# The ends of two attention mixers: when the last row sums are spread, by which way one of them goes, and which PSUM banks two late products use

## The chip, the cores and the metric

The kernel runs on one core of a Trainium2 chip. Each engine of the core (TensorE, here PE; VectorE, DVE; ScalarE, ACT; GpSimd, POOL; SyncE, SP) works through its own queue of instructions in order, and waits on semaphores for what the other engines and the DMAs deliver. The metric is the time of one execution on the device in microseconds (us); several runs are compared by their median.

## What is computed

The reference is a trunk of two layers over 1024 tokens of width 1024, in float32.

```python
for i in range(DEPTH):                      # DEPTH = 2
    h = rms_norm(x, norm_g[i])
    y = mixer_a(h, ...) if i == 0 else mixer_b(h, ...)
    x = x + y
    g = sigmoid(rms_norm(x, ple_norm_g[i]) @ ple_w_gate[i])
    x = x + g * (p[i] @ ple_w_proj[i])
return rms_norm(x, final_norm_g)
```

Both mixers have 16 heads of 64 columns. Each projects h to q, k, v and a gate, takes softmax(q k) v for each head, multiplies by silu(gate), and ends in an output projection. Mixer A attends within a window of 8 x 16 neighbours on a 16 x 64 grid, mixer B to all 1024 tokens, with four heads sharing one k and v and with norms and rotations on q and k. For this study only the very last part of each mixer matters: the softmax is left undivided through the product with v, and the sum over each row of exponentials is divided out of the result at the end.

## The kernel before

**Arithmetic.** Each float32 operand is split into a high and a low part, and a product is three matmuls (`split3`, recorded under the helper's line L321). Tokens come in 8 tiles of 128; a "half" hf is four of these tiles. The heads are worked in eight pairs.

**Four stages.** Mixer A, a dense phase (output projection in Strassen's form, `strassen_out`, then the gated projection), mixer B, and a dense phase again. The mixers use seven or eight of the eight PSUM banks in pools of their own, and the dense phase that follows takes the same eight banks afresh (four for its tiles `d`, four for `t`).

**Order of the work.** The order of all instructions is written out by hand. `mix` takes a list `att` of attention items and a list `dense` of projection items with costs, and puts dense items behind attention items so that both advance in proportion. After each attention item runs `pulse`, which moves weights along (`WQ.pump`) and counts down the list `post`: `post.add(n, f)` means that f is issued n pulses later. `later` does the same once per attention step. The last few dense items can be kept back (`hold`, HOLD = 2) and run after the last attention item, one pulse each; mixer B keeps three, of which one is used up during the last attention step. These kept items are the last of 16 "p products" (`pp_items`), which multiply the per-layer embedding by its projection: six matmuls into one PSUM bank, evacuated by ACT (L635), and stored to DRAM by a DMA from SP's queue (L636).

**Attention steps.** Mixer A has 128 steps (16 heads x 8 tiles), mixer B 128 steps (pair, half, head of the pair, tile; numbers 112 to 127 are the last pair). Step n issues the transposes of its exponentials (`f_T`: PE, then ACT L1283 for the high part PTh and DVE L1284 for the low part PTl in mixer B; L794, L799, L800 in mixer A), the exponential of a later step (`f_E`, ACT L1271 or L786, which also sums the row), the scores of a still later step (`f_S`; in mixer B DVE L1265 takes their minimum), and the product with v (`f_AV`, tile `o`; in mixer B every second step, with one PSUM bank for `o`).

**End of a head.** `head_end` (L500) runs when a head's half of `o` is complete. It issues the evacuation of `o` (ACT L548), one pulse later `join` (DVE L512), which adds the low part into Y and frees the `o` bank, and `norm` (L537), which takes reciprocals of the row sums (DVE L538, 128 x 4). The row sums lie along partitions and must be turned to lie along columns, in a 128 x 512 tile `rb`. There are two ways:

- pairs 0 to 6: `rows` (L514) transposes 128 x 32 on DVE (L516), then SP writes it to DRAM with four DMAs (L519) and reads it back, spread over the partitions, with two (L521).
- pair 7: `spread` (L524) copies the reciprocals into 128 x 512 on DVE (L525), and `across` (L528) turns that with four PE transposes (L531) into a PSUM bank (mixer A: a tile `t`; mixer B: the one bank of `o`). For the first half ACT copies the bank to `rb` (L534); for the second half it is read from PSUM.

`fin_last` (L560) then multiplies Y by the gate (DVE L561) and by the reciprocals (L565), and writes the last eighth of the dense phase's input as high (ACT L570) and low part (DVE L573). In mixer A both halves of pair 7 end after the last attention step; in mixer B the first half ends while the last eight steps run (its head ends at step 120), and the second after the last step.

**PSUM banks of the p products.** `dalloc` gives a `d` bank: mixer A has two, mixer B one. Scores have two tiles `s` (mixer A one bank each, mixer B two banks each).

Of the kernel before, what the change touches and what calls it, by code (L numbers as in the profile page):

```python
# [11 lines left out]
F32 = mybir.dt.float32  # L12
# [9 lines left out]
NT = 8  # L22
# [3 lines left out]
NH = 16  # L26
# [4 lines left out]
CA = (1.0, 0.5, 1.25, 1.0, 0.75)  # L31
CB = (1.25, 1.0, 2.0, 0.5, 1.0)
# [5 lines left out]
DT = (5, 2)  # L38
FIN = (4, 4)
HOLD = 2  # L40
# [120 lines left out]
def trunk(ctx, tc, x, wts, rpb, gains, hgains, mask, sides, rope, gain0, out):  # L161
    nc = tc.nc
    sync, act, dve, pool, pe = nc.sync, nc.scalar, nc.vector, nc.gpsimd, nc.tensor
# [154 lines left out]
    post = Later()  # L318
# [173 lines left out]
    def to_ht(pt, t, xn, cs=(0, 1)):  # L492
        for c in cs:
# [3 lines left out]
            act.activation(HTh[:, t, 4 * c:4 * c + 4], ps, AF.Copy)  # L497
            dve.tensor_tensor(HTl[:, t, 4 * c:4 * c + 4], ps, HTh[:, t, 4 * c:4 * c + 4], ALU.subtract)  # L498

    def head_end(sb, h, hf, rs, Ops, ylive, layer, gg, talloc):  # L500
        pair = h // 2
        b = (h % 2) * 64
        if h % 2 == 0:
            Y = sb.tile([128, 512], F32, name="Y", bufs=3 if layer == 0 else 2)
            rb = sb.tile([128, 512], F32, name="rb", bufs=2)
            r8 = sb.tile([128, 8], F32, name="r8", bufs=4)
            ylive[pair, hf] = (Y, rb, r8, {})
        Y, rb, r8, tail = ylive[pair, hf]
        yh = Y[b:b + 64]

        def join():
            dve.scalar_tensor_tensor(yh, Ops[0:64], 0.5, yh, op0=ALU.mult, op1=ALU.add)  # L512

        def rows():  # L514
            r8T = sb.tile([128, 32], F32, name="r8T", bufs=2)
            dve.transpose(r8T.rearrange("p (a c) -> p a c", a=4), r8[:, None].to_broadcast([128, 4, 8]))  # L516
            rD = dram.tile([8, 128], F32, name="rD", bufs=4)
            for b in range(4):
                post.add(DD[layer][1], lambda b=b: sync.dma_start(rD[:, 32 * b:32 * b + 32], r8T[32 * b:32 * b + 8]))  # L519
            for i in range(2):  # L520
                post.add(DD[layer][1], lambda i=i: sync.dma_start(  # L521
                    rb[64 * i:64 * i + 64], bass.AP(tensor=rD.tensor, offset=rD.offset + 512 * i, ap=[[0, 64], [1, 512]])))

        def spread():  # L524
            dve.tensor_copy(rb.rearrange("p (t j c) -> p t j c", t=4, j=2),  # L525
                            r8.rearrange("p (j t) -> p t j", j=2)[:, :, :, None].to_broadcast([128, 4, 2, 64]))

        def across():  # L528
            ps = talloc()
            for t in range(4):  # L530
                pe.transpose(ps[:, t], rb[:, t * 128:(t + 1) * 128], ident)  # L531
            ps = ps.rearrange("p t c -> p (t c)")
            if hf == 0:
                act.activation(rb, ps, AF.Copy)  # L534
            tail["rb"] = rb if hf == 0 else ps

        def norm():  # L537
            dve.reciprocal(r8[:, 4 * (h % 2):4 * (h % 2) + 4], rs)  # L538
            if h % 2 == 0:
                return  # L540
            if pair < 7:
                post.add(DD[layer][0], rows)
            else:
                spread()
                post.add(DT[hf], across)

# [12 lines left out]

        def fin_last():  # L560
            dve.tensor_tensor(Y, Y, G, ALU.mult)  # L561
            if "rb" not in tail:
                post.l = [e for e in post.l if e[1] is not across]
                across()
            dve.tensor_tensor(Y, Y, tail["rb"], ALU.mult)  # L565
            y3 = Y.rearrange("p (t c) -> p t c", t=4)
            ts = slice(4 * hf, 4 * hf + 4)

            def hi():
                act.activation(HTh[:, ts, 7, :], y3, AF.Copy)  # L570

            def lo():
                dve.tensor_tensor(HTl[:, ts, 7, :], y3, HTh[:, ts, 7, :], ALU.subtract)  # L573
            if hf == 0:
                post.add(3, hi)
                post.add(5, lo)
            else:
                hi()
                lo()

        def fin():
            yhi, ylo = rb.bitcast(F32R), Y.bitcast(F32R)

            def store(c, src):
                sync.dma_start(yD[layer][c][4 * hf:4 * hf + 4, :, pair, :].rearrange("t p c -> p t c"),
                               src.rearrange("p (t c) -> p t c", t=4))

            def split():
                act.activation(yhi, Y, AF.Copy)
                dve.tensor_tensor(ylo, Y, yhi, ALU.subtract)  # L590
                post.add(2, lambda: (store(0, rb), store(1, Y)))
            pool.tensor_tensor(Y, Y, G, ALU.mult)
            pool.tensor_tensor(Y, Y, rb, ALU.mult)
            if pair < 4 and hf == 1:
                post.add(YS[layer] + 2, lambda: store(0, Y))
            else:
                post.add(YS[layer], split)
        return fin_last if pair == 7 else fin
# [72 lines left out]
    def mixer_a():  # L671
        jobs = weight_sums()
        with ExitStack() as es:
# [6 lines left out]
            MK = one.tile([128, 5, 128], F32, name="MK")  # L680
            SIDE = one.tile([128, 3, 128], F32, name="SIDE")

            def dalloc():
                return pd.tile([128, 512], F32, name="d")

            def valloc():
# [2 lines left out]
            gg, ylive = {}, {}  # L689
# [69 lines left out]
            def f_S(h, j):  # L759
                k0, k1 = near(j)  # L760
                m = (k1 - k0 + 1) * 128
                n = 256
                ps = psS.tile([128, 512], F32, name="s")
                qt = QS[h][:, j * 128:(j + 1) * 128]
                ks = slice(k0 * 128, (k1 + 1) * 128)
                mm(ps[:, :m], qt, KA[h][:, ks], True, False)
                mm(ps[:, :m], qt, KB[h][:, ks], False, True)
                if j == 0:
                    RS[h] = sb.tile([128, 8], F32, name="rs", bufs=3)
                    tb = TB[h][:, 2:5:2]  # L770
# [12 lines left out]
            def f_E(h, j):  # L783
                n = 256
                sp, mn = SP[h, j]
                act.activation(sp[:, :n], sp[:, :n], AF.Exp, bias=mn, scale=-1.0, accum_out=RS[h][:, j:j + 1])  # L786

            def f_T(h, j):
                sp, _ = SP.pop((h, j))
# [199 lines left out]
            def open3():  # L989
                WQ.cap[3] = 1  # L990

            f_S(0, 0)
            f_E(0, 0)
            join(0)
# [3 lines left out]
            f_E(0, 1)  # L998
            f_S(0, 2)
            load_u(1)  # L1000
            steps = [(h, j) for h in range(NH) for j in range(NT)]

            def av_and_v(h, kb):
                fs = [(lambda: f_AV(h, kb), CA[4])]
# [4 lines left out]
            for h in range(NH):  # L1009
# [24 lines left out]
                    if h == 14 and j == OPEN3:  # L1034
                        att.append((open3, 0.0))
                if h == NH - 1:
                    att += [(lambda k=k: f_AV(NH - 1, k), CA[4]) for k in range(NT - 3, NT)]
                dense = []
                if h < NH - 1:
                    dense += qk_items(h + 1)  # L1040
# [13 lines left out]
    def mixer_b(pend):  # L1054
        with ExitStack() as es:
# [13 lines left out]
            def dalloc():  # L1069
                if pro[0]:  # L1070
                    pro[1] += 1
                    if pro[1] <= ENTRY:
                        return psS.tile([128, 1024], F32, name="s")[:, :512]
                    if pro[1] % 2 == 0:
                        return psO.tile([128, 512], F32, name="o")
                return pd.tile([128, 512], F32, name="d")

            gg, ylive = {}, {}
            KA, KB, V, QT, QST, P, RS, OP = {}, {}, {}, {}, {}, {}, {}, {}
            later = Later()  # L1080
# [187 lines left out]
            def f_E(h, hf, t):  # L1268
                ps, mn = P[h, hf, t]
                p = sb.tile([128, 1024], F32, name="P")  # L1270
                act.activation(p, ps, AF.Exp, bias=mn, scale=-1.0, accum_out=RS[h, hf][:, t:t + 1])  # L1271
                P[h, hf, t] = p

            def f_T(h, hf, t):
# [57 lines left out]
            for g in range(4):  # L1332
# [27 lines left out]
                    if YLOAD_B <= n < YLOAD_B + NT:  # L1360
                        att.append((lambda t=n - YLOAD_B: load_y(1, t), 0.0))
                if g == 3:
                    att.append((lambda: f_AV(*steps[-1]), CB[1]))
                def gates(p):
                    return [i for hf in range(2) for i in gate_items("bg", p, hf, dalloc, sb, gg)]
                dense = []
# [475 lines left out]
```

## Time and profile before

| | us |
|---|---|
| median of three runs | 1506.16 |
| lowest and highest run | 1504.79 and 1506.50 |
| profiled execution, device time | 1505.39 |
| its span from first to last instruction | 1503.6 |
| mixer A ends, first dense phase begins | about 517.7 in the span |
| mixer B ends, second dense phase begins | about 1323.1 in the span |

The profiled execution's own time is 1.8 us more than its span, and 0.77 us less than the median of the three runs.

How to read the profile: a row of the timeline gives start, duration, engine, line and operation, output tile <- input tiles, shape, and in square brackets how long the engine was idle before it and whom it waited for. `x2` means that consecutive instructions of the same kind are merged in one row. Matmuls are pipelined, so that their modelled durations overlap: six matmuls of 128 x 512, each shown with about 0.4 us, take about 1.4 us together. A row of the windows view gives, for one stretch of the span, the busy time of each engine with the number of instructions, the granted TensorE clock, the share of the DMA engines' time that was used, and GB/s.

### The profile page before, as it was taken

To read this page: it belongs to the slowest core of one execution; us is meant where nothing else is said; L and a number is where in the kernel's file an instruction comes from. 1 tells how busy PE (TensorE), PEld (TensorE's weight loads), DVE (VectorE), ACT (ScalarE), POOL (GpSimd) and SP (SyncE) were. 2 spreads that over 40 slices of the span, in tenths; PEclk is the share of its full clock that TensorE was granted. 3 is DMA by queue.
4 is the path that set the end of the run, shared out by engine and by line. 5 is a ranking of instruction groups with operands and counts; after the bars stand their busy time and mean duration, and the time that the engine had idled before them with its cause. 6 is when DMAs were issued, how large, how long until landed. Compare 5 with 4: busy or idle time off the path is not lost.

```text
span 1503.6 us, 24725 instructions
## 1 busy us (share of the span) xinstructions
PE 1480.6 (98%) x8885; PEld 1304.0 (87%) x8885; DVE 1071.6 (71%) x2042; ACT 917.2 (61%) x1866; POOL 461.0 (31%) x623
## 2 busy tenths in 40 slices
PE   8999999999999999999999999999999999999998
PEld 8888988988988887888988999989999988888886
DVE  7566476477477598756887786777877887689844
ACT  7676476477477535433567776767767777745432
POOL 1456476387265200020322222443131300000123
PEclk9999999999999999999999999999999999999999
DMA  8334374283122863262210111111101122763223
GB/s 257 126 104 131 71 178 139 64 168 100 36 89 85 326 247 99 92 206 80 77 50 22 33 51 39 47 33 44 58 28 48 38 78 66 240 234 114 69 90 135
DMA packets 91242, 157.44 MB, mean 105 GB/s; under 512 B 18160, under 2 KB 54256, under 8 KB 90608
## 3 DMA queue, kind: packets, MB, share of 16 engines
q1 hardware_dynamic: 87120, 143.53, 29.1%
q0 software_dynamic: 2560, 8.39, 3.7%
q10 hardware_dynamic: 1440, 3.94, 0.8%
q8 instruction: 71, 1.16, 0.3%
q14 instruction: 51, 0.42, 0.1%
HBM read 125.30 MB, written 50.83 MB: 117 GB/s over the span
## 4 chain that ended last, share of the span: by engine, by line
PE 51%; DVE 7%; ACT 2%; issue 1%; POOL 0%; ACTq 0%; POOLq 0%; DVEq 0%
PE d L321 25%; PE s L321 9%; PE o L321 8%; PE t L1281 7%; PE t L496 1%; DVE xn L1616 1%; PE t L321 1%; DVE X L1512 1%; DVE PTl L1284 1%; DVE HTl L1458 0%; DVE wl L235 0%; DVE mn L1265 0%; DVE wl L1410 0%; PE t L1235 0%; ACT wh L230 0%
## 5 line engine op out<-in xcount | busy, mean ns | idle before, releaser
L321 PE MATMUL d<-wh,HTh 128*128 128x256 f32 (+1 forms) x1000 | 331.8, 335 | 1.9 <-DVE X L1512 0.6
L321 PE MATMUL d<-wh,HTl 128*128 128x256 f32 (+1 forms) x1000 | 327.7, 331 | 0.4 <-DVE HTl L498 0.4
L321 PE MATMUL d<-wl,HTh 128*128 128x256 f32 (+1 forms) x1000 | 327.0, 330 | 0.3 <-DVE wl L1410 0.2
L1284 DVE TENSOR_TENSOR PTl<-t,PTh 128x512 fp32r<-128x512 f32 x256 | 164.7, 685 | 106.5 <-ACT PTh L1283 106.2
L321 PEld LDWEIGHTS d<-wh,HTh 128*128 128x128 f32 x1000 | 187.8, 189 | 22.2 <-ACT HTh L497 1.5
L321 PEld LDWEIGHTS d<-wl,HTh 128*128 128x128 f32 x1000 | 188.1, 189 | 20.0 <-DVE wl L1410 0.6
L321 PE MATMUL d<-HTh,wh 128*128 128x512 f32 x504 | 204.6, 406 | 0.0
L321 PEld LDWEIGHTS d<-wh,HTl 128*128 128x128 f32 x1000 | 187.9, 189 | 18.9 <-DVE HTl L498 0.6
L321 PE MATMUL d<-HTh,wl 128*128 128x512 f32 x504 | 198.1, 393 | 0.0
L321 PE MATMUL d<-HTl,wh 128*128 128x512 f32 x504 | 197.3, 392 | 0.0
L1271 ACT ACTIVATE P<-s,mn 128x1024 f32<-128x1024 f32 x128 | 142.7, 1115 | 47.3 <-DVE mn L1265 46.4
L1283 ACT ACTIVATE PTh<-t 128x512 fp32r<-128x512 f32 x256 | 139.2, 594 | 46.2 <-PE t L1281 45.7
L1265 DVE TENSOR_REDUCE mn<-s 128x1 f32<-128x1024 f32 x128 | 155.1, 1212 | 9.8 <-PE s L321 9.2
L804 POOL TENSOR_TENSOR PTh<-PTh,SIDE 128x256 fp32r<-128x256 f32 x96 | 81.2, 845 | 192.9 <-ACT PTh L799 192.9
L1281 PE MATMUL t<-ident,P 128*128 128x128 f32 x1024 | 134.8, 273 | 2.6 <-DVE PTl L1284 2.0
L321 PE MATMUL s<-KA,QS 128*128 128x512 f32 (+2 forms) x384 | 134.1, 403 | 1.1 <-DVE mn L778 1.1
L1281 PEld LDWEIGHTS t<-ident,P 128*128 128x128 f32 x1024 | 115.3, 140 | 12.8 <-DVE PTl L1284 6.9
L321 PE MATMUL s<-KB,QS 128*128 128x512 f32 (+2 forms) x384 | 121.5, 370 | 0.0
L235 DVE TENSOR_TENSOR wl<-wstage,wh 128x1024 fp32r<-128x1024 f32 x78 | 97.8, 1255 | 32.8 <-ACT wh L230 32.5
L321 PE MATMUL o<-PTl,V 128*128 128x256 f32 (+2 forms) x672 | 120.0, 290 | 1.1 <-DVE PTl L1284 0.6
L321 PE MATMUL o<-PTh,V 128*128 128x256 f32 (+2 forms) x672 | 118.4, 287 | 1.8 <-DVE Y L512 0.8
L321 PEld LDWEIGHTS d<-HTh,wl 128*128 128x128 f32 x504 | 94.6, 188 | 21.6
(253 smaller groups left out, 2883.3 us busy)
## 6 DMA issues: line engine op xcount, KB each, us to landing
wstage<-in_wts SPq DMA_DIRECT2D x88, 512.0 KB
pp<-ppD SPq DMA_DIRECT2D x32, 256.0 KB
X<-in_x SPq DMA_DIRECT2D x15, 512.0 KB
rb<-rD SPq DMA_DIRECT2D x56, 128.0 KB
ppD<-th SPq DMA_DIRECT2D x20, 256.0 KB
tD0t<-in_wts SPq DMA_DIRECT2D x16, 256.0 KB
tD1t<-in_wts SPq DMA_DIRECT2D x16, 256.0 KB
xD<-X SPq DMA_DIRECT2D x8, 512.0 KB
```

The source lines that it names most:

```text
L235: eng.tensor_tensor(lo[:, c:c + n], s[:, c:c + n], hi[:, c:c + n], ALU.subtract)
L321: pe.matmul(ps, a, b, start=first, stop=last, skip_group_check=True)
L496: pe.transpose(ps[:, k], xn[:, (4 * c + k) * 128:(4 * c + k + 1) * 128], ident)
L804: pool.tensor_tensor(pt[:, 3 * j - 1:3 * j + 4:4], pt[:, f1:f1 + 1].to_broadcast([128, 2, 128]), SIDE[:, :2], ALU.mult)
L1265: dve.tensor_reduce(mn, ps, axis=AX.X, op=ALU.min)
L1271: act.activation(p, ps, AF.Exp, bias=mn, scale=-1.0, accum_out=RS[h, hf][:, t:t + 1])
L1281: pe.transpose(ps[:, i], p[:, k * 128:(k + 1) * 128], ident)
L1283: act.activation(PTh[:, ks, c], ps, AF.Copy)
L1284: dve.tensor_tensor(PTl[:, ks, c], ps, PTh[:, ks, c], ALU.subtract)
L1512: dve.tensor_tensor(xt, ps, xt, op)
L1616: dve.scalar_tensor_tensor(xn, X[t], rn[m][:, i:i + 1], g1, op0=ALU.mult, op1=ALU.mult)
```

## The change

1. **Last row sums.** In both mixers, two pulses after the last exponential has been issued, `last_sums` takes the reciprocals of the last head's second half and spreads them into `rb`. `norm` then finds them there and only asks for `across`.
2. **Mixer B's last first half.** For pair 7, half 0 of mixer B, the row sums go the way of the pairs before it, through DRAM (`rows`); the copy L525, the four PE transposes L531 and the ACT copy L534 of this half are not issued.
3. **Banks of the kept p products.** Once the last product with v is reached, `dalloc` counts its calls: in mixer A the second kept p product gets a bank of the scores `s`, in mixer B the first and third do (with two left there, the first).

```diff
+    def last_sums(rs, ylive):
+        _, rb, r8, tail = ylive[NH // 2 - 1, 1]
+        dve.reciprocal(r8[:, 4:8], rs)
+        dve.tensor_copy(rb.rearrange("p (t j c) -> p t j c", t=4, j=2),
+                        r8.rearrange("p (j t) -> p t j", j=2)[:, :, :, None].to_broadcast([128, 4, 2, 64]))
+        tail["sums"] = True
+
     def head_end(sb, h, hf, rs, Ops, ylive, layer, gg, talloc):
...
         def norm():
+            if "sums" in tail and h % 2:
+                post.add(DT[hf], across)
+                return
             dve.reciprocal(r8[:, 4 * (h % 2):4 * (h % 2) + 4], rs)
             if h % 2 == 0:
                 return
-            if pair < 7:
+            if pair < 7 or layer == 1 and hf == 0:
                 post.add(DD[layer][0], rows)
+                tail["rb"] = rb
             else:
                 spread()
                 post.add(DT[hf], across)
```

In mixer A:

```diff
+            end = [0]
+
             def dalloc():
+                if end[0]:
+                    end[0] += 1
+                    if end[0] == 1 + HOLD:
+                        return psS.tile([128, 512], F32, name="s")
                 return pd.tile([128, 512], F32, name="d")
...
                 act.activation(sp[:, :n], sp[:, :n], AF.Exp, bias=mn, scale=-1.0, accum_out=RS[h][:, j:j + 1])
+                if (h, j) == steps[-1]:
+                    post.add(2, lambda: last_sums(RS[h][:, 4:8], ylive))
...
-                    att += [(lambda k=k: f_AV(NH - 1, k), CA[4]) for k in range(NT - 3, NT)]
+                    def last_av(k):
+                        end[0] = k == NT - 1
+                        f_AV(NH - 1, k)
+                    att += [(lambda k=k: last_av(k), CA[4]) for k in range(NT - 3, NT)]
```

In mixer B:

```diff
+                if end[0]:
+                    end[0] += 1
+                    if end[0] % 2 == 0:
+                        return psS.tile([128, 1024], F32, name="s")[:, :512]
                 return pd.tile([128, 512], F32, name="d")
...
                 act.activation(p, ps, AF.Exp, bias=mn, scale=-1.0, accum_out=RS[h, hf][:, t:t + 1])
+                if (h, hf, t) == steps[-1]:
+                    post.add(2, lambda: last_sums(RS[h, hf], ylive))
...
                 if g == 3:
-                    att.append((lambda: f_AV(*steps[-1]), CB[1]))
+                    def last():
+                        end[0] = 1
+                        f_AV(*steps[-1])
+                    att.append((last, CB[1]))
```

The list `steps` of mixer A is also built a few lines earlier than before, since `f_E` now reads it.

More of the change, by code (lines that the diff above doesn't have):

```diff
@@ L990, in open3 @@
                 WQ.cap[3] = 1
+            steps = [(h, j) for h in range(NH) for j in range(NT)]
             f_S(0, 0)
@@ L1000, in mixer_a @@
             load_u(1)
-            steps = [(h, j) for h in range(NH) for j in range(NT)]
             def av_and_v(h, kb):
@@ L1075, in dalloc @@
                         return psO.tile([128, 512], F32, name="o")
+                if end[0]:
+                    end[0] += 1
+                    if end[0] % 2 == 0:
+                        return psS.tile([128, 1024], F32, name="s")[:, :512]
                 return pd.tile([128, 512], F32, name="d")
+            end = [0]
             gg, ylive = {}, {}
```

## Prediction

> **What bounds the kernel now.** I read the page first, then the waits of PE over the whole span, then the timeline of both mixers' ends, and last the windows behind them.
>
> ```profile
> PE 1480.6 (98%) x8885; PEld 1304.0 (87%) x8885; DVE 1071.6 (71%) x2042; ACT 917.2 (61%) x1866; POOL 461.0 (31%) x623
> PE o L531 <- DVE Y L512: 0.8, 1, 0.8
> PE o L321 <- DVE Y L512: 0.8, 2, 0.5
> PE d L321 <- DVE X L1512: 0.6, 1, 0.6
> PE t L531 <- DVE rb L525: 0.5, 1, 0.5
> ```
>
> PE is busy for 1480.6 of 1503.6 us, so that all its gaps together are 23 us. The change can only take PE work away at one place (four transposes) and close gaps at the two ends. Two waits of the list belong to it by name, L531 on L512 (0.8) and L531 on L525 (0.5); shorter ones follow below. The whole matter is therefore one of one to three microseconds. The question for each is whether it is passed on to the end, or given back to DVE, which the Strassen stage behind each mixer keeps busy.
>
> **Part 1 and 3, mixer A.** The rows below are the timeline of its end: the last exponential, the first kept p product's last matmul, the spread of the second half's sums, its turn on PE, the second kept product, and the first product of the dense phase.
>
> ```profile
> 506.97 0.51 ACT L786 ACTIVATE sp<-sp,mn 128x256 f32<-128x256 f32 x1
> 509.31 0.42 DVE L800 TENSOR_TENSOR PTl<-t,PTh 128x256 fp32r<-128x256 f32 x1 [1.35 <-ACT PTh L799]
> 514.19 0.40 PE L321 MATMUL d<-wh,wl 128*128 128x512 f32 x1
> 514.47 0.43 DVE L525 COPY rb<-r 128x512 f32<-128x512 f32 x1
> 515.05 0.63 PE L531 MATMUL t<-ident,rb 128*128 128x128 f32 x4 [0.46 <-DVE rb L525]
> 515.43 0.48 PE L321 MATMUL d<-wh,KA 128*128 128x512 f32 x1
> 517.11 0.60 ACT L635 ACTIVATE G<-d 128x512 f32<-128x512 f32 x1 [1.88 <-PE d L321]
> 517.75 0.50 PE L321 MATMUL d<-wh,HTh 128*128 128x512 f32 x1 [0.25 <-ACT G L635]
> 519.17 0.69 DVE L565 TENSOR_TENSOR Y<-Y,rb 128x512 f32<-128x512 f32 x1 [2.85 <-ACT rb L534]
> 521.96 0.69 DVE L573 TENSOR_TENSOR HTl<-Y,HTh 128x512 fp32r<-128x512 f32 x1 [0.70 <-ACT HTh L570]
> 526.00:579.00 53.00, 52.36 (x229) 42.55 (x228) 52.31 (x77) 22.94 (x37) 0.00 (x0) 1.00 0.52 188
> ```
>
> The transposes start at 515.05 because the copy ends at 514.90. PE could have begun about a quarter of a microsecond behind the matmul of 514.19 (six such matmuls take 1.4 us), at 514.4. So the copy costs PE at least the 0.46 that the profile names and at most 515.05 - 514.4 = 0.65; I take 0.6, since the weights of the transposes were held up too.
>
> After the change the copy and its reciprocal come two pulses behind the exponential of 506.97, which is the last of the mixer. DVE then sits idle for 1.35 us before 509.31. The copy is 0.43, and a 128 x 4 reciprocal is at most the 0.20 that a 128 x 32 transpose takes below. Cover 1.35 against 0.63: they cost nothing. Without that cover, they would cost DVE at most 0.63 and PE nothing at that place, since PE's next product with v waits for other steps.
>
> The second kept product then starts 0.6 earlier, and with it all that hangs on its end in ACT's queue: its evacuation (517.11), a weight split, L534, and through it DVE's L565 at 519.17 (which waits 2.85 for L534), L570, and L573 at 521.96. From there DVE runs without a pause worth naming: 52.31 of the 53 us from 526 to 579. That run's start sets when the stage ends, and PE waits for it there (0.6 on L1512, above). So mixer A gives **0.6**.
>
> The other bank saves PE the wait of 0.25 at 517.75. Nothing else is held by it, and PE only reaches the end of DVE's run 0.25 earlier and waits there: I count **0**, with 0.25 to 0.4 as the upper end. That a p product in a scores bank waits for something new has no row; the last reader of these banks on ACT and DVE is before 508, and the product starts after 514, so that I take nothing for it, and as its upper end the 0.25 saved.
>
> **Part 2, mixer B's first half.** Here the turn on PE is removed. The timeline around it:
>
> ```profile
> 1289.41 1.03 PE L1281 MATMUL t<-ident,P 128*128 128x128 f32 x8
> 1290.54 0.68 DVE L512 SCALAR_TENSOR_TENSOR Y<-o,Y 64x512 f32<-64x512 f32 x1
> 1291.28 0.66 PE L531 MATMUL o<-ident,rb 128*128 128x128 f32 x4 [0.84 <-DVE Y L512]
> 1291.69 0.71 PE L321 MATMUL s<-KA,QS 128*128 128x512 f32 x2
> 1292.77 1.28 DVE L1284 TENSOR_TENSOR PTl<-t,PTh 128x512 fp32r<-128x512 f32 x2
> 1293.55 0.60 ACT L534 ACTIVATE rb<-o 128x512 f32<-128x512 f32 x1
> 1295.28 1.12 ACT L1271 ACTIVATE P<-s,mn 128x1024 f32<-128x1024 f32 x1 [0.37 <-DVE mn L1265]
> 1296.91 1.09 ACT L1283 ACTIVATE PTh<-t 128x512 fp32r<-128x512 f32 x2 [0.43 <-PE t L1281]
> 1300.78 1.29 DVE L1284 TENSOR_TENSOR PTl<-t,PTh 128x512 fp32r<-128x512 f32 x2 [0.81 <-ACT PTh L1283]
> 1301.98 1.22 DVE L1265 TENSOR_REDUCE mn<-s 128x1 f32<-128x1024 f32 x1
> 1303.83 0.69 DVE L565 TENSOR_TENSOR Y<-Y,rb 128x512 f32<-128x512 f32 x1
> 1306.34 1.29 DVE L1284 TENSOR_TENSOR PTl<-t,PTh 128x512 fp32r<-128x512 f32 x2 [1.82 <-ACT PTh L1283]
> 1310.16 1.19 PE L321 MATMUL o<-PTh,V 128*128 128x256 f32 x8 [0.52 <-DVE Y L512]
> ```
>
> PE waits 0.84 for the `o` bank, which L512 frees, and spends 1291.69 - 1291.28 = 0.41 on the transposes: the scores of step 123 can start **1.25** earlier. ACT loses L534 (0.60) and DVE a copy of 0.43; DVE gains a 0.20 transpose.
>
> Does PE keep the 1.25? The low parts of step 121 (1292.77) stand on DVE behind a weight split, and do not move; nor does the exponential of 1295.28, which waits for the minimum behind them. So ACT comes to L1283 of step 122 when that exponential ends, 0.43 earlier, not 1.25. DVE then works through low parts, minimum, low parts, minimum without its gap of 0.81 at 1300.78, and is 0.43 + 0.81 = 1.24 earlier at 1301.98. PE's own work in between is at no place nearer than that. At 1310.16 PE waits for DVE's L512 once more (0.52, the longer of the two of L321 above), and that L512 follows the same chain. So 1.2 of the 1.25 is left there: **1.2**.
>
> The DRAM way adds six DMAs to SP's queue, and L565 waits for their landing with all of DVE's queue behind it (the low parts of 1306.34 first). Its price by the pair before:
>
> ```profile
> 1260.28 0.20 DVE L516 STREAM_TRANSPOSE r8T<-r 128x32 f32<-128x32 f32 x1
> 1260.51 1.29 SPq L519 DMA_DIRECT2D rD<-r8T  x4
> 1263.38 1.09 SPq L521 DMA_DIRECT2D rb<-rD  x2
> 1267.15 1.30 POOL L593 TENSOR_TENSOR Y<-Y,rb 128x512 f32<-128x512 f32 x1 [6.85 <-DMA rb<-rD]
> 1260.50:1267.10 6.60, 6.60 (x40) 5.72 (x40) 3.51 (x4) 3.86 (x8) 0.00 (x0) 1.00 0.48 154
> 1290.80:1297.00 6.20, 5.72 (x38) 4.99 (x39) 3.98 (x5) 5.24 (x10) 0.00 (x0) 1.00 0.98 339
> ```
>
> From the first store to the use of rb: 1267.15 - 1260.51 = 6.6 us. The new transpose comes behind L512, which itself moves up by the copy's 0.43: 1290.54 - 0.43 + 0.68 + 0.20 = 1291.0, and the first store 0.2 later, at 1291.2. Landing by this row: 1297.8. But the DMA engines are at 0.98 there, against 0.48. If the share doubles the time, the landing is at 1291.2 + 13.2 = 1304.4; that is the upper end. L565 is reached at 1303.83 - 1.2 = 1302.6. I take 1299, nearer to the row, since most of the 6.6 us is the 2.87 between first store and first load and the 3.77 after, in which little data moves: **0**. On SP the loads hold the queue until about 1295, where the store of the next p product stands behind them; its data are ready about then (the evacuation of a product has to come after 1293.55 today), so it loses nothing worth counting. The Trainium skill, page DMA: Bandwidth & Descriptors, section Latency and other measured facts, gives an access to HBM as 0.2 us on average and 2 us at high load. By it, an estimate, both legs of this way could take 1.8 us longer here, with the landing at about 1301.4. No row shows the legs under such a load, and the sum is the same by the row and by the page.
>
> **Parts 1 and 3, mixer B's end.**
>
> ```profile
> 1317.29 1.29 DVE L1284 TENSOR_TENSOR PTl<-t,PTh 128x512 fp32r<-128x512 f32 x2 [1.10 <-ACT PTh L1283]
> 1320.90 0.66 PE L531 MATMUL o<-ident,rb 128*128 128x128 f32 x4
> 1320.97 0.60 ACT L635 ACTIVATE th<-d 128x512 f32<-128x512 f32 x1 [0.84 <-PE d L321]
> 1321.62 0.50 PE L321 MATMUL d<-wh,KA 128*128 128x512 f32 x1
> 1325.48 0.69 DVE L573 TENSOR_TENSOR HTl<-Y,HTh 128x512 fp32r<-128x512 f32 x1 [3.11 <-ACT HTh L570]
> ```
>
> The second half's sums move into DVE's gap of 1.10 before 1317.29 (0.63 of work). They are not late today: the turn at 1320.90 waits for L512 to free the bank. So **0**. The last p product needs the one `d` bank, which L635 holds until 1321.57; with the other bank it starts when the transposes end, 1320.90 + 0.41 = 1321.31: **0.3**. Its end sets ACT's next steps and L573, so DVE's start in the Strassen stage moves with it.
>
> **Sum.** 0.6 + 1.2 + 0.3 = 2.1 us. The profiled execution took 1505.39, so it would take 1503.3. It stands 0.77 below the median of the three runs; taken from the median, 1506.16 - 2.1 = **1504.1 us**, 0.14% less. About 0.2%, or 3.0 us, is what a measurement of this kernel can tell from no change (the three runs span 1.7), so my forecast is a gain below that.
>
> **The rivals.**
>
> *Swallowed in mixer B.* ACT and DVE between 1292 and 1310 could be no earlier at all, so that PE waits longer at 1310.16 and only 0.3 of B is left: 0.9 in all, 1505.3. For it: the exponential of 1295.28 does not move. Against it: the gaps of 0.43, 0.81 and 1.82 behind it, which are waits on PE or on its followers. 0.14.
>
> *All that is saved is kept.* In A 0.65 with the 0.4 of the bank, in B 1.4 and 0.35 with the pieces of other waits: 2.8 to 3.3, about 1503.1. Against it: the run of DVE from 526 to 579. 0.18.
>
> *Lost later.* The Strassen stage could be paced by something that does not move, a load landing. Then nothing is left: 1506.2. Against it: no wait of PE in the list names a DMA there. 0.08.
>
> *Slower: rb lands late.* Decided where L565 stands on DVE: from 1302.6 there are 1.8 us until the low parts of today's 1306.34, so a landing after 1304.4 moves everything behind it by what it is late, and after 1306.5 more is lost than the 2.1 gained. That is 15.3 us behind the first store, against 6.6 at half the DMA load. A landing at 1309 gives 2.5 slower, 1508.7. 0.08: the load of 0.98 speaks for it, the 4.8 us between 1297.8 and 1302.6 against.
>
> **How the numbers follow.** 0.52 is left for the forecast. A gain over 3.0 us needs the case where all is kept and half of its chance (0.09), or the forecast with a sixth of its chance for the scatter of medians (0.09), and 0.02 from the rest: faster 0.20. Slower by over 3.0: 0.05, most of the late landing. Within: 0.75. The range reaches down to 1503.1 less 1.1 of scatter, 1502.0, and up past the lost case, 1506.2 and 0.4: 1506.6; what it leaves out is mainly the late landing.
>
> **What would show it.** Right: no transposes L531 into `o` near 1290 and scores of step 123 right behind the transposes of step 121; no wait of L531 on L525; L573 of mixer A about 0.6 earlier and of mixer B about 2.1; PE's wait on L1512 behind mixer A 0.9 instead of 0.6. Wrong: DVE waiting for the DMA of rb at L565; a wait at 1310 of more than 0.7; a DVE run behind mixer A that begins earlier and ends where it did.

## The result, and the profile after

| | before | after |
|---|---|---|
| median, runs beside each other (22 of each), us | 1508.05 | 1504.69 |
| lowest and highest, us | 1504.79 and 1514.23 | 1503.08 and 1509.15 |
| profiled execution, device time, us | 1505.39 | 1504.51 |
| its span, us | 1503.6 | 1502.7 |

The ratio of the times is 0.9983, with a 95% interval of 0.9976 to 0.9990: 0.17% faster, or 2.6 us (1.5 to 3.6). That is a gain, and by its middle one just below the 0.2% that the prediction took as the bound, with an interval that reaches over it. A second timing of the changed kernel, told below as after_again, gave 0.9995 (0.9986 to 1.0004). The two intervals have only the gains from 1.5 to 2.1 us in common. The traces say it better.

PE's row of the page's first part, busy time, share of the span and instructions:

```profile
PE 1478.8 (98%) x8881; PEld 1302.5 (87%) x8881; DVE 1071.7 (71%) x2042; ACT 917.3 (61%) x1865; POOL 460.5 (31%) x623
```

PE has 4 instructions less, the turned transposes of mixer B's first half, ACT one, and DVE as many as before (a transpose for a copy).

The two spans can't simply be subtracted: after's profile is already 1.28 us later at a point near 473 us that the change doesn't touch. The places to measure from, here called marks, are two DVE transposes of row sums that the change leaves alone: the last one of mixer A, and in mixer B that of the first half of pair 6, the last but one before the change. The following rows are DVE's timeline of the kernel before: mixer A's mark, the first normalized tile xn behind the Strassen stage, and mixer B's mark.

```profile
472.18 0.21 DVE L516 STREAM_TRANSPOSE r8T<-r 128x32 f32<-128x32 f32 x1
...
588.83 2.48 DVE L1616 SCALAR_TENSOR_TENSOR xn<-X,rn,gain 128x1024 f32<-128x1024 f32 x2
...
1225.66 0.20 DVE L516 STREAM_TRANSPOSE r8T<-r 128x32 f32<-128x32 f32 x1
```

And the same three rows after the change (line numbers have moved by 7 to 32):

```profile
473.46 0.21 DVE L523 STREAM_TRANSPOSE r8T<-r 128x32 f32<-128x32 f32 x1
...
589.44 2.48 DVE L1648 SCALAR_TENSOR_TENSOR xn<-X,rn,gain 128x1024 f32<-128x1024 f32 x2
...
1226.37 0.20 DVE L523 STREAM_TRANSPOSE r8T<-r 128x32 f32<-128x32 f32 x1
```

From mixer A's mark to xn: 588.83 - 472.18 = 116.65 before and 589.44 - 473.46 = 115.98 after, 0.67 less. From mixer B's mark to the end of the span: 1503.6 - 1225.66 = 277.94 and 1502.7 - 1226.37 = 276.33, 1.61 less. From mixer A's mark to the end: 1031.42 and 1029.24, **2.18 us less**, where the sum of the prediction was 2.1. These stretches repeat to 0.1 us from one execution to the next (the long one to about 0.3); the whole time doesn't, for reasons that lie ahead of mixer A's mark; the main one is found below.

The timeline of mixer A's end after the change:

```profile
509.16 0.17 DVE L502 RECIPROCAL r<-rs 128x4 f32<-128x4 f32 x1
509.33 0.74 POOL L823 TENSOR_TENSOR PTl<-PTl,SIDE 128x256 fp32r<-128x256 f32 x1
509.37 0.98 DVE L503 COPY rb<-r 128x512 f32<-128x512 f32 x1
510.49 0.43 DVE L819 TENSOR_TENSOR PTl<-t,PTh 128x256 fp32r<-128x256 f32 x1
...
515.48 0.40 PE L321 MATMUL d<-wh,wl 128*128 128x512 f32 x1
515.71 0.60 PE L538 MATMUL t<-ident,rb 128*128 128x128 f32 x4
516.07 0.48 PE L321 MATMUL s<-wh,KA 128*128 128x512 f32 x1
517.75 0.60 ACT L646 ACTIVATE G<-s 128x512 f32<-128x512 f32 x1 [1.24 <-PE s L321]
518.39 0.19 PEld L321 LDWEIGHTS d<-wh,HTh 128*128 128x128 f32 x1 [0.49 <-ACT G L646]
518.39 0.50 PE L321 MATMUL d<-wh,HTh 128*128 128x512 f32 x1 [0.25 <-ACT G L646]
```

The turn L538 (L531 before) now follows the first kept product at once, 0.23 us behind its last matmul's start instead of 0.86. But the first dense product, the last row, still waits 0.25 for the evacuation of the second kept product, although that product now lies in a bank of `s`.

The timeline of mixer B's last first half:

```profile
1290.12 1.03 PE L1310 MATMUL t<-ident,P 128*128 128x128 f32 x8
...
1290.90 0.71 PE L321 MATMUL s<-KA,QS 128*128 128x512 f32 x2
...
1292.34 1.23 DVE L235 TENSOR_TENSOR wl<-wstage,wh 128x1024 fp32r<-128x1024 f32 x1 [0.89 <-ACT wh L230]
...
1293.48 0.21 DVE L523 STREAM_TRANSPOSE r8T<-r 128x32 f32<-128x32 f32 x1
...
1293.72 1.30 SPq L526 DMA_DIRECT2D rD<-r8T  x4
...
1298.23 1.09 SPq L528 DMA_DIRECT2D rb<-rD  x2
...
1303.19 0.69 DVE L576 TENSOR_TENSOR Y<-Y,rb 128x512 f32<-128x512 f32 x1
...
1304.07 0.60 ACT L646 ACTIVATE th<-d 128x512 f32<-128x512 f32 x1 [0.22 <-PE d L321]
1304.56 0.62 ACT L581 ACTIVATE HTh<-Y 128x512 fp32r<-128x512 f32 x1
...
1305.08 1.08 ACT L1312 ACTIVATE PTh<-t 128x512 fp32r<-128x512 f32 x2
...
1305.71 1.29 DVE L1313 TENSOR_TENSOR PTl<-t,PTh 128x512 fp32r<-128x512 f32 x2 [1.83 <-ACT PTh L1312]
```

The scores of step 123 (1290.90) stand right behind the transposes of step 121, with nothing turned on PE between them, and L576 (L565 before) has no bracket: it doesn't wait for rb. Mixer B's end:

```profile
1315.67 0.43 DVE L503 COPY rb<-r 128x512 f32<-128x512 f32 x1
...
1316.65 1.29 DVE L1313 TENSOR_TENSOR PTl<-t,PTh 128x512 fp32r<-128x512 f32 x2 [0.55 <-ACT PTh L1312]
...
1320.26 0.66 PE L538 MATMUL o<-ident,rb 128*128 128x128 f32 x4
...
1320.67 0.48 PE L321 MATMUL d<-wh,KA 128*128 128x512 f32 x1
...
1324.49 0.69 DVE L584 TENSOR_TENSOR HTl<-Y,HTh 128x512 fp32r<-128x512 f32 x1 [2.77 <-ACT HTh L581]
```

The last p product (1320.67) follows the turn after 0.41 us, not after 0.72 as before.

### The profile page after: what moved, and what is told of

Read it like the earlier page. It is cut to its first block, busy times and chain, and to the rows that moved or that the text cites. A ratio compares the mean times of both kernels' runs of the same rounds, so it can differ in the third digit from the quotient of the medians.

```text
span 1502.7 us, 24726 instructions
## 1 busy us (share of the span) xinstructions
PE 1478.8 (98%) x8881; PEld 1302.5 (87%) x8881; DVE 1071.7 (71%) x2042; ACT 917.3 (61%) x1865; POOL 460.5 (31%) x623
## 4 chain that ended last, share of the span: by engine, by line
PE 52%; DVE 6%; ACT 2%; issue 1%; POOL 0%; POOLq 0%; ACTq 0%; DVEq 0%
PE d L321 26%; PE s L321 9%; PE o L321 8%; PE t L1310 7%; PE t L496 1%; DVE xn L1648 1%; PE t L321 1%; DVE X L1544 1%; DVE PTl L1313 1%; DVE HTl L1490 0%; DVE mn L1292 0%; DVE wl L1442 0%; PE t L1262 0%; DVE wl L235 0%; ACT wh L230 0%
```

## The experiments

My theory: the gain is the sum of three local ones, about 0.65, 1.2 and 0.4; in mixer A it is DVE's Strassen run that passes it on, and whatever PE alone saves there is lost at PE's next wait for DVE; and the DRAM way has only little room. The rivals: the parts don't add up, since one covers for another; the gain in mixer A comes from PE, so that freeing PE further gives more; and rb may land much later at no cost.

The timed ratios carry intervals of about 0.1% to either side, as large as the parts themselves. So each experiment is decided by the stretches between the marks, taken from its own trace like those above. The kernel before has one trace; the runs that leave a part out repeat its stretches at the place of that part (116.60 and 116.61 to xn, 277.88 to the end):

| kernel | ratio to before (95%) | A mark to xn, us | B mark to end, us | A mark to end, us |
|---|---|---|---|---|
| before | | 116.65 | 277.94 | 1031.42 |
| after | 0.9983 (0.9976 to 0.9990) | 115.98 | 276.33 | 1029.24 |
| after_again | 0.9995 (0.9986 to 1.0004) | 115.98 | 276.40 | 1029.14 |
| sums_only | 0.9994 (0.9984 to 1.0004) | 115.95 | 277.88 | 1030.83 |
| dram_only | 0.9994 (0.9985 to 1.0003) | 116.60 | 276.71 | 1030.41 |
| banks_only | 1.0002 (0.9993 to 1.0011) | 116.61 | 277.50 | 1031.14 |
| o_bank | 0.9983 (0.9974 to 0.9992) | 115.96 | 276.37 | 1029.11 |
| early_turn | 0.9985 (0.9975 to 0.9994) | 115.29 | 276.39 | 1028.69 |
| early_turn_o | 0.9998 (0.9986 to 1.0009) | 114.99 | 276.44 | 1028.16 |
| rows_late5 | 0.9990 (0.9979 to 1.0001) | 115.98 | 276.78 | 1029.93 |
| rows_late9 | 1.0011 (1.0000 to 1.0023) | 115.98 | 279.31 | 1032.45 |
| early_table | 0.9977 (0.9966 to 0.9988) | 115.98 | 276.37 | 1029.38 |
| all_together | 0.9978 (0.9969 to 0.9987) | 115.43 | 276.40 | 1028.89 |

**One part at a time.** sums_only keeps part 1 alone: the condition of `rows` is the old one, and `end[0]` is never set.

```diff
-            if pair < 7 or layer == 1 and hf == 0:
+            if pair < 7:
...
-                        end[0] = k == NT - 1
...
-                        end[0] = 1
```

> Only part 1: both mixers' last row sums spread early; the turn on PE in mixer B's first half and all banks are as before. Theory (each part gives its own term): at the end of mixer A the transposes L531 no longer wait, and everything behind them stands 0.6 us earlier than it would; mixer B's end is unchanged, since its last turn waits for the o bank anyway; 0.6 us of the program's time, ratio about 0.9996. Rival (mixer A's gain comes from the other bank of the second kept product): nothing moves, ratio 1.000, and the wait of 0.5 turns into one of the same size on something else.

Measured: 0.70 less in mixer A, 0.06 less behind mixer B's mark. Part 1 works in mixer A and nowhere else.

dram_only keeps part 2 alone: the two calls of `post.add(2, lambda: last_sums(...))` are taken out, and the lines that set `end[0]`.

> Only part 2: mixer B's last first half goes through DRAM. Theory: the scores behind step 121's transposes start 1.4 us earlier, 1.2 to 1.3 of it is left at the product with v near 1310, and as much at the program's end: ratio about 0.9991. The wait of the transposes on the spread in mixer A (0.5) and the late start of mixer B's last p product (0.3) stay. Rival (ACT and DVE swallow it by 1310): 0.3 or less is left, the wait near 1310 grows from 0.5 to 1.5, ratio 0.9998.

Measured: 0.05 less in mixer A, 1.23 less behind mixer B's mark. One row of its PE timeline shows the old wait back in place, for the copy, in the turn behind the first kept product:

```profile
521.15 0.63 PE L538 MATMUL t<-ident,rb 128*128 128x128 f32 x4 [0.46 <-DVE rb L532]
```

banks_only keeps part 3 alone: no `last_sums`, and the old condition of `rows`.

> Only part 3: the kept p products' banks. Theory: mixer B's last p product starts 0.3 us earlier and the program ends 0.3 earlier; in mixer A the first dense product still waits 0.25 for the evacuation of the second kept product, as in the changed kernel; ratio 0.9998. Rival (the bank is what mixer A's end hung on): the first dense product of layer 0 starts 0.3 to 0.6 earlier, ratio 0.9995.

Measured: 0.04 less in mixer A, 0.44 less behind mixer B's mark. So the parts give 0.70, 1.23 and 0.44 at their own places, and together 0.67 and 1.61 (1.23 + 0.44 = 1.67): they add up, and the rival that one covers for another falls. None of the three can be told from no change by its own timing.

**What bounds mixer A's end.** o_bank puts mixer A's second kept product in a bank of the pool of `o` in place of one of `s`:

```diff
-                        return psS.tile([128, 512], F32, name="s")
+                        return psO.tile([128, 512], F32, name="o")
```

> The changed kernel with one thing more: mixer A's second kept p product goes into a bank of the pool o, which the dense phase's second pool takes over, in place of one of the scores' banks. Theory: the first dense product's wait of 0.25 on that evacuation is for the whole of the banks that the dense phase's first pool takes over, and so goes away; PE is then 0.3 to 0.4 earlier there, waits 0.9 in place of 0.6 for DVE's L1544 behind the Strassen stage, and the program is no faster than the changed kernel (ratio to the kernel before about 0.9984). Rival A (the wait is for ACT's last evacuation wherever it lies): the wait of 0.25 stays. Rival B (PE is what bounds that stage): the program ends another 0.3 to 0.4 us earlier.

Measured: PE's first dense product comes 44.43 us behind the mark instead of 44.93, without a wait, and xn at 115.96 instead of 115.98. PE is half a microsecond ahead, and gives all of it back to DVE, though at another wait than the one that was expected. The list of PE's waits behind mixer A (waiting tile, what released it, us in total, times, longest) in the kernel after:

```profile
PE d L321 <- DVE X L1544: 0.6, 1, 0.6
PE t L496 <- DVE xn L1648: 0.4, 1, 0.4
PE d L321 <- DVE wl L1442: 0.2, 1, 0.2
```

and in o_bank:

```profile
PE d L321 <- DVE wl L1442: 0.7, 1, 0.7
PE d L321 <- DVE X L1544: 0.6, 1, 0.6
PE t L496 <- DVE xn L1648: 0.4, 1, 0.4
```

The wait for `wl` grows by 0.5, just what PE had won. What does set xn is DVE's own run, whose first sum is this row of the kernel after:

```profile
526.08 0.69 DVE L1468 TENSOR_TENSOR S<-HTh 128x512 f32<-128x512 f32 x1
```

From the start of this sum to xn pass 63.36 us here (526.08 to 589.44), and 63.35 to 63.39 in all thirteen traces, wherever PE stands. Counted from the mark, the sum comes at 53.26 in the kernel before, at 52.62 in after and at 52.60 in o_bank.

That the bank in `s` is waited for because the dense phase's first pool takes over the place of both `d` and `s`, and not that of `o`, fits both traces; it is argued from them and wasn't tried further.

The other way round, early_turn brings DVE's run forward: the first half's turn is issued 3 pulses behind the join, not 5.

```diff
-DT = (5, 2)
+DT = (3, 2)
```

> The changed kernel with mixer A's first half turned two pulses sooner (DT of 3 in place of 5), so that its transposes stand ahead of the second kept p product and not behind it. Theory (DVE's run behind mixer A sets the end of that Strassen stage, and its start hangs on the second kept product through ACT's queue): L541 is copied ahead of that product's evacuation, L584 starts 2 us or more earlier, and PE's waits in the stage (0.2 on wl, 0.6 on L1544, 0.4 on xn) shrink to nearly none; against it the first dense product starts 0.4 later, since it still waits for the same evacuation without the transposes in between. Net 0.5 to 0.9 faster than the changed kernel, from mixer A's end to the first step of mixer B. Rival (the stage's end hangs on ACT, POOL or loads): L584 is earlier and the waits stay as they are; 0.4 slower.

Measured: L584, the end of the dense phase's input, comes 46.80 us behind the mark instead of 49.13, 2.33 earlier; xn is only 0.69 earlier. Three rows of its timeline show what came between:

```profile
520.46 0.50 PE L321 MATMUL d<-wh,HTh 128*128 128x512 f32 x1 [0.69 <-ACT G L646]
...
521.91 1.29 DVE L584 TENSOR_TENSOR HTl<-Y,HTh 128x512 fp32r<-128x512 f32 x2 [1.24 <-ACT HTh L581]
...
527.02 0.69 DVE L1468 TENSOR_TENSOR S<-HTh 128x512 f32<-128x512 f32 x1 [1.54 <-DMA ppD<-G]
```

DVE now runs into a DMA: the first sum of its run waits 1.54 for the store of the last p product, out of the buffer G. It comes at 51.91, 0.71 earlier than in after, and xn follows it after 63.38. PE's wait at the first product has grown from 0.25 to 0.69, and yet xn is earlier; PE's waits for `wl` and on L1544 are gone. So an earlier start of DVE's run does bring the stage forward, and an earlier PE alone doesn't; the rival that PE bounds falls.

early_turn_o has both edits.

> The same with mixer A's second kept product in a bank of the pool o as well, so that the first dense product does not wait for its evacuation. Theory: PE and DVE are both earlier now, and what o_bank gave back to DVE's run is kept: 1.0 to 1.4 faster than the changed kernel, ratio to the kernel before about 0.9975. Rival (as before): no faster than the changed kernel.

Measured: xn 0.99 earlier than after, and 1.08 us less from mark to end. DVE's first sum comes at 51.61; its wait for the store out of G is 1.24 instead of 1.54. The 1.08 is the best of all, and yet its timing, 0.9998, is one of the worst and missed the 0.9975 that was expected. What decides the timing lies elsewhere.

**How late may rb land?** rows_late5 and rows_late9 issue `rows` of pair 7 that many pulses later.

```diff
-                post.add(DD[layer][0], rows)
+                post.add(DD[layer][0] + (5 if pair == 7 else 0), rows)
```

> The changed kernel with the DRAM way of mixer B's last first half begun five pulses later. Theory (L576 is reached at about 1303.2 and DVE has 1.8 us of rest behind it): the first store goes out 2.5 to 4 us later, rb lands near or up to 2 us after the point where L576 needs it, and PE loses 0 to 0.3 us. Rival (the changed kernel's landing is already the last thing at L576): every microsecond of delay is lost, 2.5 to 4 us slower than the changed kernel.

> The changed kernel with the DRAM way of mixer B's last first half begun nine pulses later, ahead of L576 by only two attention items. Theory: the first store goes out 6 to 7 us later, rb lands 3 to 5 us after L576 is reached, the 1.8 us of rest on DVE are used up and 1.5 to 3 us are lost against the changed kernel: about as slow as the kernel before or slower. Rival (DVE's and PE's slack there is larger than one gap): less than 0.5 us is lost.

In rows_late5 the timeline shows DVE waiting for the DMA at the place that the prediction named:

```profile
1305.31 0.69 DVE L576 TENSOR_TENSOR Y<-Y,rb 128x512 f32<-128x512 f32 x1 [1.22 <-DMA rb<-rD]
```

In rows_late9, with the steps that follow it on ACT and PE:

```profile
1310.11 0.69 DVE L576 TENSOR_TENSOR Y<-Y,rb 128x512 f32<-128x512 f32 x1 [3.03 <-DMA rb<-rD]
1310.84 0.63 ACT L581 ACTIVATE HTh<-Y 128x512 fp32r<-128x512 f32 x1 [2.33 <-DVE Y L576]
1311.37 1.07 ACT L1312 ACTIVATE PTh<-t 128x512 fp32r<-128x512 f32 x2
1312.73 1.25 PE L1310 MATMUL t<-ident,P 128*128 128x128 f32 x8 [1.70 <-DVE PTl L1313]
```

Counted from mixer B's mark, L576 comes at 76.82 in after, 77.89 in rows_late5 (1.07 later) and 80.42 in rows_late9 (3.60 later). The end moves by 276.78 - 276.33 = 0.45 and by 2.98 (0 to 0.3 and 1.5 to 3 were expected). What is lost is each time the delay of L576 less 0.62: that is all the room there is behind L576, and from there on it costs a microsecond for a microsecond. The room can be read from ACT: in after L576 ends at 1303.88, and ACT, busy with the evacuation L646, starts L581 at 1304.56, 0.68 later; in rows_late9 L581 starts 0.04 behind L576's end. The rival that rb may land late for nothing falls.

**Where the scatter comes from.** after_again is the changed kernel once more, beside the next one.

> The changed kernel once more, to stand beside the next two on the same chip. Every theory: from the last row transpose of mixer A to the first of mixer B 327.5 to 327.7 us, from the last but two of mixer B to the end 276.3; the first row transpose of all anywhere between 105 and 112, since that is where the runs scatter; ratio 0.998 to 0.999.

Its stretches are those of after within 0.1 us. But the first of all these row transposes, near 106 us, is at 105.14 to 111.22 in the thirteen traces, and what runs ahead of it is the same in all but two of the kernels. The difference is mostly one wait of PE near 55 us, for the minimum of mixer A's scores; the row of PE's timeline in after:

```profile
55.15 0.44 PE L321 MATMUL s<-KA,QS 128*128 128x384 f32 x1 [1.70 <-DVE mn L795]
```

in sums_only:

```profile
55.12 0.64 PE L321 MATMUL s<-KA,QS 128*128 128x384 f32 x1 [2.21 <-DVE mn L794]
```

and in dram_only:

```profile
56.81 0.69 PE L321 MATMUL s<-KA,QS 128*128 128x384 f32 x1 [3.12 <-DVE mn L795]
```

On POOL, in dram_only, the table L765 stands 7.86 us for a load, and the low parts of the mixer's weights stand in POOL's queue behind it:

```profile
43.93 2.14 POOL L765 TENSOR_TENSOR tb<-MK,u 128x128 f32<-128x128 f32 x5 [7.86 <-DMA u<-U]
```

early_table issues this table after the last weight split ahead of the mixer, so that POOL does the split first:

```diff
                 if t == 6:
                     load_u(0)
-                    table(0)
                 if t in (4, NT - 1):
                     WQ.pump(True)
                     WQ.settle()
+                if t == NT - 1:
+                    table(0)
```

> The changed kernel with the first head's position table built on POOL behind the low parts of the last weight split of the start, in place of ahead of them. Theory (the scatter between runs is the landing of the table's last load, which holds POOL, through POOL the weights, and through them the third scores of mixer A; a wait there of over 2 us also lowers the granted clock): PE's wait on the minimum of the first scores, 0.8 to 3.1 us in the runs so far, falls below 1, the clock stays at 1.00 from 40 to 60 us, and the program is 1 to 4 us faster than the changed kernel in the mean, ratio 0.996 to 0.9975. Rival (the weights' own loads set that wait): no change in the wait and the time.

Measured: the wait near 55 us is 0.4, the mark comes at 105.26, and the table no longer waits:

```profile
46.59 4.03 POOL L765 TENSOR_TENSOR tb<-MK,u 128x128 f32<-128x128 f32 x5
```

The median is 1503.00 (lowest and highest 1502.37 and 1505.12), beside 1505.15 (1503.68 and 1508.77) of after_again on the same chip. The stretches behind mixer A's mark are unchanged. So a wait ahead of everything studied here moves the time by as much as the whole change. That it moves with this queue is shown; what makes the load's landing vary wasn't tried.

It isn't the only place that scatters. From the first row transpose to mixer A's mark eleven traces take 366.0 to 367.1 us, rows_late5 367.9 and early_turn_o 368.9. In these two PE waits 1.75 and 1.74 near 319 us for POOL, where it waits 0.37 in after. Why POOL is late there wasn't tried.

all_together is early_turn_o with early_table.

> The changed kernel with all three additions: the earlier turn of mixer A's first half, the second kept product in a bank of the pool o, and the first table behind the weights on POOL. Theory: the gains add, 1.0 to 1.3 at mixer A's end and 1 to 4 at the start, 2 to 5 us faster than the changed kernel, ratio to the kernel before 0.995 to 0.997. Rival (only the local waits move): no faster than the changed kernel.

Measured: 1503.04 (1502.08 to 1505.51), ratio 0.9978, no different from early_table alone, so that the gains did not add up in the time as the theory had it. Mark to end is 0.35 less than in after, not the 1.08 of early_turn_o: DVE's wait for the store out of G is 1.68 where early_turn_o had 1.24, its first sum comes at 52.06, and xn is 0.55 earlier.

## Why the prediction was right, and where its steps were not

The time was 1504.69 against 1504.1, but the median before was also higher in the later runs (1508.05 against 1506.16), so that the gain is what compares: 2.1 predicted, 2.6 (1.5 to 3.6) by the first timing, 0.8 (-0.6 to 2.1) by the second, 2.18 by the traces. That 1504.69 lies so near 1504.1 is thus luck in part. The likeliest case was the right one, with a sum that was right because its terms were: each measured at or a little above what was written, with some 0.17 of the first not seen at mixer B.

*The last sums in mixer A, 0.6: right.* 0.67 at xn, 0.70 with this part alone, and L584 is 0.65 nearer to the mark (49.13 against 49.78), where 0.6 was written. The path was the one worked out: DVE's run, of fixed length, starts 0.64 earlier. The cover was tighter than worked out: the copy took 0.98, not 0.43, and with its reciprocal ends at 510.35, just ahead of the low parts at 510.49. POOL was at work from 509.33 to 510.07 at the same time; where the copy took 0.43, at 512.99 in mixer A and at 1315.67 in mixer B, POOL was idle. That POOL held it up fits these rows and wasn't tried. Some 0.17 of the gain is no longer there at mixer B's begin (from mark A to B's first transpose 328.02 before, 327.52 after), within the scatter of that stretch.

*The other bank in mixer A, 0: the number right, its working wrong.* The prediction said that the wait of 0.25 goes, and that PE would then wait 0.9 instead of 0.6 at L1512. Neither is so: the wait stayed, and with it the 0.6. For the bank of `s` the 0 was luck, since nothing was saved that could be handed back. o_bank did remove it, and showed that the count of 0 was sound: PE lost its half microsecond at an earlier wait for DVE, that for `wl`.

*Mixer B's first half, 1.2: right.* Counted from the mark, the scores of step 123 come 1.50 earlier, where 1.25 was worked out, the product with v near 1310 1.34, and the end 1.23 (dram_only). The exponential of 1295.28 didn't move (69.62 and 69.71 behind the mark), and the high parts behind it came 0.43 earlier, both as worked out. The wait near 1310 is 0.50 and not more.

*The landing: right in its sign, wrong in two sizes.* The transpose was placed right behind L512, with the first store at 1291.2. The transpose came at 1293.48 and the store at 1293.72, 1.8 us later by the mark: on DVE a weight split (1292.34) stood before it, and that waited 0.89 for ACT. The way itself took longer too: from the first store to the first load 4.51 us (1293.72 to 1298.23) where the pair before had 2.87. The Trainium skill (DMA: Bandwidth & Descriptors, Latency and other measured facts) lets an HBM access grow from 0.2 to 2 us at high load; the 1.64 that this leg grew by agrees with the 1.8 that the prediction worked out from it. The second leg hardly grew: 4.18 in rows_late5 and 3.72 in rows_late9, where the landing is seen, against 3.77. An estimate from these puts rb's landing in after at 1302.0 to 1302.4, some 1 us before L576 and not the 3.6 us that 1299 against 1302.6 had left. So the 0 came true with little to spare. That no row shows the legs under such a load was wrong: the trace of before has two such pairs in mixer A, from 187.51 and from 305.96, with DMA shares of 0.89 and 0.87, first legs of 4.56 and 5.14 and second legs of 4.08 and 4.17; by them the landing comes out, as an estimate, at 1299.8 to 1300.5. On SP the loads held the queue until 1299.3 and not 1295; no row from there to mixer B's end names a wait for a DMA.

*The slower rival: its price by the microsecond right, its point wrong.* 1.8 us were to rest on DVE, taken from the idle time ahead of the next low parts (1.82). Measured: 0.62. The idle time was read as slack, and it isn't: those low parts wait for PTh on ACT, and in ACT's queue L581, which needs L576, stands ahead of it (1304.56, then 1305.08). Once L576 is more than 0.62 later, it pushes L581, PTh and so the end of the idle time along with it. By the point on record rows_late5 would have cost nothing; it cost 0.45. The chance of 0.08 was too small for a margin of this kind.

*Mixer B's end, 0.3: right, a little too small.* The step from the turn to the product shrank by 0.31, as worked out; in banks_only the last low part of the dense phase's input is 0.36 earlier by the mark and the end 0.44.

*What a matmul's row names.* The idle time in its brackets was less than the loss at three places: 0.46 named and 0.63 to 0.65 lost at the turn in mixer A, 0.25 and 0.50 at the bank, 1.25 worked out with the 0.84 named and 1.50 lost at step 123. The weights' row, with its 0.49, is right for the bank; at the turn in mixer A it names 0.87, too much.

*Swallowed in mixer B, all kept, lost later.* The first is refuted by the 1.23, the third by the 2.18 that arrives at the end. All kept was 2.8 to 3.3; the traces give less, since DVE holds mixer A's end.

## What to carry to other kernels

Idle time ahead of an instruction is room for a delay only if what ends that idle time doesn't hang on the thing that is delayed: follow the releaser's own queue one step back before counting the gap as slack. In a stage where one engine runs without a pause, what moves its start arrives at the end, and what moves another engine is handed back at the next wait. For a change of two microseconds in fifteen hundred, compare stretches between marks in the traces, and look for the waits that make the whole time scatter before timing anything.

## What the runs showed of the hardware

The cost of the wait near 55 us is more than its length. The windows view of after, just behind the wait (engines in the order PE, PEld, DVE, ACT, POOL; then the clock):

```profile
56.00:58.00 2.00, 2.00 (x10) 1.63 (x10) 1.06 (x2) 1.91 (x4) 0.89 (x3) 1.00 0.60 221
```

The same stretch of sums_only:

```profile
56.00:58.00 2.00, 2.00 (x6) 1.54 (x5) 1.10 (x2) 1.91 (x4) 0.83 (x2) 0.50 0.65 231
```

And a stretch of dram_only, where the wait ended at 56.81:

```profile
58.00:60.00 2.00, 2.00 (x6) 1.57 (x5) 1.40 (x2) 1.79 (x3) 1.72 (x4) 0.50 0.50 174
```

Behind a wait of 1.70 the clock stays at 1.00; at 2.21 it is halved for 3.4 us, and at 3.12 for 6.8, with 6 matmuls in 2 us where 10 ran before. So the 6 us between early_table's first row transpose (105.26) and dram_only's (111.22) are worked out as 2.7 of longer wait and 3.4 of half clock. The other traces fit no simple rule by the length of the wait. 2.17 (early_turn) and 2.96 (rows_late9) were each followed by 3.4 us of half clock. 1.69 (banks_only) and 1.75 (rows_late5, near 319 us) were followed by none, but 1.74 at that same place in early_turn_o by 3.4 us, here with the four microseconds behind it:

```profile
319.32 0.45 PE L321 MATMUL o<-PTh,V 128*128 128x384 f32 x1 [1.74 <-POOL PTh L823]
```

```profile
320.00:324.00 4.00, 4.00 (x13) 3.46 (x14) 0.76 (x3) 0.87 (x3) 4.00 (x9) 0.60 0.83 107
```

The Trainium skill (TensorE: Matmul & The Clock Gate, HAM oscillation — how this bites in real kernels) gives idle gaps over about 3.4 us as what to avoid; its throttled rate of half agrees with the 0.50 here, but waits of 2.17 to 3.12 us were enough in these runs, and once one of 1.74.

How long a small store takes until it can be read back rises with the load. From the first store to the first load of the row sums passed 2.18 us with a DMA share of 0.02 in between (rows_late9), 2.87 with 0.49 (the pair before, in the kernel before), 4.05 with 0.54 (rows_late5) and 4.51 with 0.85 (after). In the kernel before, 21 of 28 such legs took 2.17 to 2.36, at shares of at most 0.35, and the two longest 4.56 and 5.14 at 0.89 and 0.87; but one took 3.16 at 0.02, so that the load isn't all. The leg behind it, from load to landing, took 3.72 to 4.18 us in the runs named, at shares of 0.47 to 0.61, and 3.46 to 4.38 for the pair before in all thirteen traces.
